# The QKV stage of a fused encoder: rotation of both halves at once on the vector engine, x's norm folded into the head norms, float32 sums, a first weight in parts

## The chip, the core and the metric

The kernel runs on one core of a Trainium2 chip, as one program. Five engines work side by side, each through its own queue in order: TensorE multiplies matrices into PSUM, the vector engine (DVE in the rows) and ScalarE (ACT) work element by element, GpSimd (POOL) does the same more slowly, and SyncE (SP) issues the transfers. They wait for one another by semaphores. The time is that of the device for the whole program in microseconds (us); a profile is one execution, recorded instruction by instruction.

## The reference

The trunk has two layers over 1024 tokens of 1024 features: grouped-query attention and an MLP, then bidirectional gated linear attention and an MLP, and a last norm. The change touches the first step, where q and k are made:

```python
hn = rmsnorm(h, norm_mix[0])                 # y = h * rsqrt(mean(h*h) + EPS) * g
q, k, v = split(hn @ w_qkv)                  # 16 heads of q, 4 of k and v, 64 features each
q = rmsnorm(q.reshape(B, S, 16, 64), q_g)    # over each head's 64 features
k = rmsnorm(k.reshape(B, S, 4, 64), k_g)
# axial rotation: of each 32 features the first 16 are x1, the others x2
rotated = concat([x1 * c - x2 * s, x2 * c + x1 * s])
```

The softmax over q k, its product with v, and everything behind it stay as they are.

## The kernel before

All data are float32. A projection keeps the accuracy by splitting both operands into a high part (`fp32r`, written by a ScalarE cast) and a low part (the difference, on the vector engine): three matmuls, high by high, high by low, low by high (`mm3`, L108 to L111), for each of eight 128-row pieces of the contraction (`proj`, L113), so 24 matmuls of 512 columns. `split` (L95) and `load_w` (L99) make the parts of a weight; `gain_split` (L172) makes those of x with the norm's gain, but without x's root mean square. That factor is one number per token and is put in later.

x lies transposed: features on partitions, tokens along the row, in two halves of 512 tokens. Five tiles of q and k (`qk_tile`, L293), k's four heads first (t = 4) and then four heads of q at a time, each have two weights: one gives the first members of the rotated pairs (`pab[0]`, in the rows `qa`), the other the second (`qb`). So a half-tile is two projections, 48 matmuls, and there are ten half-tiles. For each, ScalarE squares both results, the vector engine adds the squares (`SumSquares`, L137), the sum is split into high and low (`sqh`, `sql`), and two matmuls with the block matrix `blk` (L164, L165) sum over the 32 partitions of each head. `products` (L318) does the rotation's four multiplications, three of them on GpSimd, with tables of cosine and sine that `x_norm` (L225) has already multiplied by x's inverse root. `rotate` (L330) multiplies the head's sum by x's inverse mean square (`xq`, L334), takes the inverse root by logarithm, exponential and one Newton step (`newton`, L124 to L135), multiplies it in (L337), splits the result, and SP writes it to DRAM, from where the score stage reads it.

`rope_late` holds each half-tile's `rotate` back until the next half-tile's projections are issued (`rope_end`, L314), so in TensorE's queue a sum stands behind 48 other matmuls. `hooks` (L232) puts x's norms, the transposes that give the inverse root by token (`by_token`, L182), and v's weights in between. `v_tiles` (L345) then makes v in eight tiles of 24 matmuls of 256 columns, with the last two `rotate` and the first head's maxima (`max_step`, L273) among them. The scores start behind it. The order within each engine's queue is fixed when the program is built, by a scheduler that moves instructions a little against the code; PSUM's banks are four for projections (`a`), two for maxima (`b`), two for sums (`c`).

The same `newton` is used by every norm of the program.

Of the kernel before, what the change touches and what calls it, by code (L numbers as in the profile page):

```python
# [41 lines left out]
NCH = S // P  # L42
LEAD = 22
LAG = 3


C_MIX0, C_MLP0, C_MIX1, C_MLP1, C_FIN, C_QA, C_QB, C_KA, C_KB, C_OUT, NCOL = 0, 8, 16, 24, 32, 40, 41, 42, 43, 44, 46
# [2 lines left out]
def trunk_kernel(tc, xT, wqk, wv, wo, win0, wout0, gqk, gv, gvz, gr, gate, gwo, win1, wout1, cols, rope, cmat, yT):  # L50
# [5 lines left out]
    with ExitStack() as top:  # L56
# [19 lines left out]

        epst = const.tile([P, 1], F32, name="epst")
        nc.vector.memset(epst, EPS)

        PS_BUFS = {"a": 4, "b": 2, "c": 2}  # L80

# [10 lines left out]
        def bank(tag):  # L92
            return psum.tile([P, HN], F32, tag=tag, name="ps_" + tag, bufs=PS_BUFS[tag])
# [27 lines left out]
        def halves(n):  # L121
            return [[None, None] for _ in range(n)]

        def newton(x, n, out=None):  # L124

            w = x.shape[-1]
            r0 = env.tmp.tile([P, HN], F32, tag="rs_r", name="rs_r")[:, :w]
            nc.scalar.activation(out=r0, in_=x, func=AF.Ln, bias=epst, scale=1.0 / n)  # L128
            nc.scalar.activation(out=r0, in_=r0, func=AF.Exp, scale=-0.5)  # L129
            t = env.tmp.tile([P, HN], F32, tag="rs_t", name="rs_t")[:, :w]  # L130
            nc.vector.scalar_tensor_tensor(out=t, in0=r0, scalar=1.0 / n, in1=r0, op0=ALU.mult, op1=ALU.mult)  # L131
            nc.vector.scalar_tensor_tensor(out=t, in0=x, scalar=n * EPS, in1=t, op0=ALU.add, op1=ALU.mult)  # L132
# [59 lines left out]
        with ExitStack() as at:  # L192
# [6 lines left out]
            rx2 = pool.tile([P, 2, HN], F32, name="rx2")  # L199
            rt = const.tile([P, NCH], F32, name="rt")  # L200
            xstack = at.enter_context(ExitStack())
            xpool = pool_of(xstack, "xpool", 16)
            wk = [load_w(wqk[8])]
            for half in range(2):
                for k in range(KT):
                    xr[k][half] = xpool.tile([P, HN], F32, tag="xr", name="xr")
                    nc.sync.dma_start(out=xr[k][half], in_=xT[k][:, HALF[half]])
                if half == 0:
                    wk.append(load_w(wqk[9]))
# [4 lines left out]
            xsums = [SumSquares(nc.vector) for _ in range(2)]  # L214
            wq = [load_w(wqk[i]) for i in range(2)]

            def x_squares(half):
# [12 lines left out]

            x_squares(0)
            x_squares(1)  # L232
# [55 lines left out]
            blk = pool.tile([P, P], F32R, name="blk")  # L288
            blk_f = pool.tile([P, HN], F32, tag="t2", name="blk_f")[:, :P]
            nc.sync.dma_start(out=blk_f, in_=rope[:, 2 * S :])  # L290
            nc.scalar.copy(out=blk, in_=blk_f)

            def qk_tile(t, w=None):  # L293
                w = w or [load_w(wqk[2 * t]), load_w(wqk[2 * t + 1])]
                ga, gb = (C_KA, C_KB) if t == 4 else (C_QA, C_QB)
                for half in range(2):
                    pab = [proj("a", w[i], x, half) for i in range(2)]
                    if hooks:
                        hooks.pop(0)()
                    rope_end()  # L300
                    sums = SumSquares(nc.vector)
                    for ps in pab:
                        sums.add(ps)
                    ab = []
# [5 lines left out]
                    rope_late.append(partial(rotate, t, half, sums, ab, None if t == 4 else products(half, *ab)))  # L310

            rope_late = []

# [1 line left out]
                if rope_late:  # L315
                    rope_late.pop()()

            def products(half, a, b):  # L318
                cc, ss = tabs[:, 0, HALF[half]], tabs[:, 1, HALF[half]]
                out = []  # L320
                for i, (u, v, op) in enumerate(((a, b, ALU.subtract), (b, a, ALU.add))):
                    t1 = pool.tile([P, HN], F32, tag=f"t1{i}", name="t1", bufs=2)
                    t2 = pool.tile([P, HN], F32, tag="t2", name="t2")
# [3 lines left out]
                    out.append(t1)  # L327
                return out

            def rotate(t, half, sums, ab, out):  # L330
                sl = HALF[half]
                out = out or products(half, *ab)
                xq = pool.tile([P, HN], F32, tag="xq", name="xq")
                nc.vector.tensor_tensor(out=xq, in0=sums.total(blk), in1=rx2[:, half], op=ALU.mult)  # L334
                r = newton(xq, 1)
                for i, t1 in enumerate(out):
                    nc.vector.scalar_tensor_tensor(out=t1, in0=t1, scalar=(0.25 if t == 4 else 0.03125), in1=r, op0=ALU.mult, op1=ALU.mult)  # L337
                    hi = pool.tile([P, HN], F32R, tag=f"qo{i}", name="qoh")
                    lo = pool.tile([P, HN], F32R, tag=f"qo{2 + i}", name="qol")
                    split(hi, lo, t1)  # L340
                    dst = kv_dram if t == 4 else q_dram[t]
                    nc.sync.dma_start(out=dst[i, :, sl], in_=hi.bitcast(F32))
                    nc.sync.dma_start(out=dst[2 + i, :, sl], in_=lo.bitcast(F32))

            def v_tiles():  # L345
                for c in range(NCH):
# [928 lines left out]
```

## Time and profile before

| | us |
|---|---|
| timed runs | 2353.15, 2357.78, 2358.01 |
| median | 2357.78 |
| profiled execution | 2352.89 |
| its span, first to last instruction | 2350.8 |
| first score matmul | 178.09 |
| last matmul of the ninth half-tile's sum starts | 140.42 |

The page of the profile shows TensorE busy for 98% of the span, the vector engine 76%, ScalarE 57%, GpSimd 14%. Matmuls overlap, so TensorE's busy time counts some stretches in which it could have taken more; what it really spends per matmul is the distance between two starts. In the fence rows further down, a row of the timeline begins with the start in us and the duration, and a bracket at its end tells how long the engine stood idle before and what released it.

### The profile page before, as it was taken

The page shows a single profiled execution, that of the slowest core. Times are in us where ns is not written, and L with a number is a line of the kernel's source. Part 1 is how long each engine was busy: PE and PEld are TensorE (multiplying, and loading weights), DVE is VectorE, ACT ScalarE, POOL GpSimd, SP SyncE. Part 2 cuts the span into 40 slices and gives each one's busy share as a digit, 9 for nine tenths or more (in the row PEclk, how much of TensorE's full clock was granted, in tenths as well). Part 3 has the DMA queues.
Part 4 walks back from the last instruction along what each step waited for, and adds up shares of the span by engine and source line. Part 5 has one row for each costly group of instructions (what it writes and reads, how often), then busy time and mean ns, then how long its engine had stood idle before and what let it go on. Part 6 is the DMA issues. An engine that isn't in the chain of part 4 may idle for free. (4 is left out here: it accounts for less than half of the span.)

```text
span 2350.8 us, 29858 instructions
## 1 busy us (share of the span) xinstructions
PE 2292.8 (98%) x10710; PEld 1898.6 (81%) x10710; DVE 1777.5 (76%) x2502; ACT 1341.4 (57%) x2386; POOL 333.2 (14%) x267
## 2 busy tenths in 40 slices
PE   8889999999999999999999999999999999999996
PEld 6677777777878888888888888898878888888885
DVE  8999999995786556888776767667696655897785
ACT  7458999994465555433344865655455555543343
POOL 2444444443000000000012000000100000000003
PEclk9999999999999999999999999999999999999998
DMA  4442112104445456954422121125625545965422
GB/s 173 135 146 64 42 41 52 30 14 165 132 160 180 152 175 228 320 166 160 153 99 81 47 74 54 55 72 187 220 91 194 177 152 182 331 204 177 154 89 72
DMA packets 157796, 317.50 MB, mean 135 GB/s; under 512 B 15048, under 2 KB 17872, under 8 KB 157520
## 3 DMA queue, kind: packets, MB, share of 16 engines
q1 hardware_dynamic: 157648, 315.60, 40.2%
q8 instruction: 84, 1.38, 0.2%
q14 instruction: 64, 0.52, 0.1%
HBM read 223.20 MB, written 92.27 MB: 134 GB/s over the span
## 5 line engine op out<-in xcount | busy, mean ns | idle before, releaser
L97 DVE TENSOR_TENSOR wl<-raw,wh 128x1024 fp32r<-128x1024 f32 x293 | 361.0, 1232 | 198.4 <-ACT wh L96 197.0
L96 ACT CAST wh<-raw 128x1024 fp32r<-128x1024 f32 x293 | 307.4, 1049 | 327.7 <-PE ps_a L466 130.6
L96 ACT CAST hh<-hst 128x512 fp32r<-128x512 f32 x224 | 134.9, 618 | 246.1 <-PE ps_a L467 112.4
L147 POOL TENSOR_TENSOR sq<-sq 128x512 f32<-128x512 f32 x35 | 54.6, 1560 | 1373.7 <-ACT sq L145 772.6
L400 POOL TENSOR_TENSOR pl<-p,ph 128x512 fp32r<-128x512 f32 x128 | 178.9, 1397 | 190.4 <-ACT p L397 136.4
L465 PE MATMUL ps_a<-xh,wh 128*128 128x512 f32 x512 | 199.6, 391 | 2.5 <-ACT xh L96 2.5
L467 PE MATMUL ps_a<-xh,wl 128*128 128x512 f32 x512 | 199.8, 391 | 1.8 <-DVE wl L97 1.8
L97 DVE TENSOR_TENSOR hl<-hst,hh 128x512 fp32r<-128x512 f32 x224 | 153.1, 703 | 62.9 <-ACT hh L96 62.1
L466 PE MATMUL ps_a<-xl,wh 128*128 128x512 f32 x512 | 200.5, 392 | 0.0
L465 PE MATMUL ps_a<-hh,wh 128*128 128x512 f32 x512 | 199.3, 389 | 1.1 <-ACT h L505 1.1
L466 PE MATMUL ps_a<-hl,wh 128*128 128x512 f32 x512 | 199.3, 389 | 0.6 <-DVE hl L97 0.6
L467 PE MATMUL ps_a<-hh,wl 128*128 128x512 f32 x512 | 199.2, 389 | 0.0
L396 ACT ACTIVATE ph<-ps_a 128x512 fp32r<-128x512 f32 x248 | 149.0, 601 | 22.2 <-PE ps_a L390 19.7
L397 ACT ACTIVATE p<-ps_a 128x512 f32<-128x512 f32 x256 | 153.1, 600 | 1.0 <-POOL pl L400 0.2
L465 PE MATMUL ps_b<-xh,wh 128*128 128x512 f32 x384 | 149.5, 389 | 0.2 <-DVE s L560 0.2
L467 PE MATMUL ps_b<-xh,wl 128*128 128x512 f32 x384 | 149.4, 389 | 0.0
L466 PE MATMUL ps_b<-xl,wh 128*128 128x512 f32 x384 | 149.4, 389 | 0.0
L277 DVE TENSOR_REDUCE mx<-ps_b 128x1 f32<-128x512 f32 x181 | 121.9, 682 | 7.6 <-PE ps_b L276 5.5
L505 ACT ACTIVATE s<-s 128x512 f32<-128x512 f32 x96 | 60.6, 631 | 105.9 <-DVE s L560 105.9
L465 PEld LDWEIGHTS ps_a<-xh,wh 128*128 128x128 f32 x512 | 96.4, 189 | 23.2 <-ACT xh L96 3.3
L467 PEld LDWEIGHTS ps_a<-xh,wl 128*128 128x128 f32 x512 | 96.5, 188 | 23.1 <-DVE wl L97 2.7
L465 PEld LDWEIGHTS ps_a<-hh,wh 128*128 128x128 f32 x512 | 96.1, 188 | 21.8 <-ACT h L505 1.7
(280 smaller groups left out, 6038.0 us busy)
## 6 DMA issues: line engine op xcount, KB each, us to landing
raw<-in_win_dram SPq DMA_DIRECT2D x80, 512.0 KB, 3.8
raw<-in_wout_dram SPq DMA_DIRECT2D x80, 512.0 KB, 3.9
hst<-hid_dramFalse SPq DMA_DIRECT2D x56, 512.0 KB, 3.8
hst<-hid_dramTrue SPq DMA_DIRECT2D x56, 512.0 KB, 3.5
q<-q_dram SPq DMA_DIRECT2D x96, 128.0 KB, 2.9
hid_dramFalse<-s SPq DMA_DIRECT2D x48, 256.0 KB, 2.1
hid_dramFalse<-t SPq DMA_DIRECT2D x48, 256.0 KB, 3.1
hid_dramTrue<-s SPq DMA_DIRECT2D x48, 256.0 KB, 2.0
```

The source lines that it names most:

```text
L96: nc.scalar.copy(out=hi, in_=src)
L97: (leng or nc.vector).tensor_tensor(out=lo, in0=src, in1=hi.bitcast(F32), op=ALU.subtract)
L147: self.eng.tensor_tensor(out=sq, in0=self.acc, in1=sq, op=ALU.add)
L277: nc.vector.tensor_reduce(out=mx[h][:, half * 8 + c : half * 8 + c + 1], in_=ps, axis=AX.X, op=ALU.max, negate=True)
L396: nc.scalar.activation(out=phh, in_=ps, func=AF.Exp)
L397: nc.scalar.activation(out=p, in_=ps, func=AF.Exp)
L400: (nc.vector if c % 2 == 0 else nc.gpsimd).tensor_tensor(out=pll, in0=p, in1=phh.bitcast(F32), op=ALU.subtract)
L465: nc.tensor.matmul(ps, wh, xh, start=start and i == 0, stop=False, skip_group_check=not start)
L466: nc.tensor.matmul(ps, wh, xl, start=False, stop=False, skip_group_check=not start)
L467: nc.tensor.matmul(ps, wl, xh, start=False, stop=i == len(parts) - 1, skip_group_check=not start)
L505: nc.scalar.activation(out=t, in_=src, func=AF.Relu)
```

## The change

`newton`: the square of the root is taken on ScalarE instead of the vector engine, with an epsilon that can be given. `products` and `rotate`: both members of a pair lie side by side in one tile (`u`, `t1`, `t2`), and each of the two tables multiplies both at once on the vector engine; GpSimd has no part in it. The tables are no longer multiplied by x's norm. Instead of dividing by it, the head's sum gets an added term: 64 times epsilon times x's mean square, in the matmul's sum (`xe`, in two float32r parts, with `ones`). The block sum itself is one float32 matmul on the unsplit squares. Gains take the factors (`gneg`). The two members leave in one transfer per part. At the start, eight matmuls on constants are issued, and k's first weight is loaded and split in four parts of 256 columns between x's first four tiles.

```diff
+WARM = 8
@@
+        epsq = const.tile([P, 1], F32, name="epsq")
+        nc.vector.memset(epsq, EPS * EPS)
+        nc.vector.tensor_scalar_mul(gneg[:, C_QA : C_QB + 1], gneg[:, C_QA : C_QB + 1], 0.125)
@@ newton
-        def newton(x, n, out=None):
+        def newton(x, n, out=None, eps=EPS, bias=epst):
-            nc.scalar.activation(out=r0, in_=x, func=AF.Ln, bias=epst, scale=1.0 / n)
+            nc.scalar.activation(out=r0, in_=x, func=AF.Ln, bias=bias, scale=1.0 / n)
             nc.scalar.activation(out=r0, in_=r0, func=AF.Exp, scale=-0.5)
-            nc.vector.scalar_tensor_tensor(out=t, in0=r0, scalar=1.0 / n, in1=r0, op0=ALU.mult, op1=ALU.mult)
-            nc.vector.scalar_tensor_tensor(out=t, in0=x, scalar=n * EPS, in1=t, op0=ALU.add, op1=ALU.mult)
+            nc.scalar.activation(out=t, in_=r0, func=AF.Square, scale=n ** -0.5)
+            nc.vector.scalar_tensor_tensor(out=t, in0=x, scalar=n * eps, in1=t, op0=ALU.add, op1=ALU.mult)
@@ start
-            wk = [load_w(wqk[8])]
+            warm = bank("c")
+            for _ in range(WARM):
+                nc.tensor.matmul(warm[:, :P], ones_f, ones_f, start=True, stop=True)
+            raw = env.raw.tile([P, D], F32, tag="raw", name="raw")
+            wk = [(wpool.tile([P, D], F32R, tag="wh", name="wh"), wpool.tile([P, D], F32R, tag="wl", name="wl"))]
             for half in range(2):
                 for k in range(KT):
+                    if half == 0 and k < 4:
+                        q = slice(k * 256, k * 256 + 256)
+                        nc.sync.dma_start(out=raw[:, q], in_=wqk[8][:, q])
+                        split(wk[0][0][:, q], wk[0][1][:, q], raw[:, q])
@@ x_squares
-                xsums[half].parts(*[pool.tile([P, HN], F32R, tag=f"qo{2 * half + i}", name="xsq") for i in range(2)])
+                xe[half] = [pool.tile([P, HN], F32R, name=f"xe{half}{i}") for i in range(2)]
+                e = pool.tile([P, 2, HN], F32, tag="t2", name="xe")[:, 0]
+                nc.scalar.activation(out=e, in_=xsums[half].acc, func=AF.Copy, scale=64 * EPS / D)
+                split(*xe[half], e)
+                xsq = pool.tile([P, 2, HN], F32R, tag="qol" if half else "qoh", name="xsq")
+                xsums[half].parts(xsq[:, 0], xsq[:, 1])
@@ x_norm
-                tab = tabs[:, :, HALF[half]]
-                nc.vector.tensor_tensor(out=tab, in0=tab, in1=rx[:, half : half + 1].to_broadcast([P, 2, HN]), op=ALU.mult)
-                nc.scalar.activation(out=rx2[:, half], in_=rx[:, half], func=AF.Square, scale=0.0625)
@@ qk_tile
-                    for ps, g, nm in ((pab[0], ga, "qa"), (pab[1], gb, "qb")):
-                        u = pool.tile([P, HN], F32, tag=nm, name=nm, bufs=2)
-                        nc.scalar.activation(out=u, in_=ps, func=AF.Copy, scale=colt[:, g : g + 1])
-                        ab.append(u)
-                    sums.parts()
+                    u = pool.tile([P, 2, HN], F32, tag="u", name="u", bufs=2)
+                    for i, ps in enumerate(pab):
+                        g = (C_KA if t == 4 else C_QA) + i
+                        nc.scalar.activation(out=u[:, i], in_=ps, func=AF.Copy, scale=gneg[:, g : g + 1])
@@ products
-                for i, (u, v, op) in enumerate(((a, b, ALU.subtract), (b, a, ALU.add))):
-                    (nc.gpsimd if i else nc.vector).tensor_tensor(out=t1, in0=u, in1=cc, op=ALU.mult)
-                    nc.gpsimd.tensor_tensor(out=t2, in0=v, in1=ss, op=ALU.mult)
-                    nc.vector.tensor_tensor(out=t1, in0=t1, in1=t2, op=op)
+                for i, t in enumerate((t1, t2)):
+                    nc.vector.tensor_tensor(out=t, in0=u, in1=tabs[:, i : i + 1, HALF[half]].to_broadcast([P, 2, HN]), op=ALU.mult)
+                nc.vector.tensor_tensor(out=t1[:, 0], in0=t1[:, 0], in1=t2[:, 1], op=ALU.subtract)
+                nc.vector.tensor_tensor(out=t1[:, 1], in0=t1[:, 1], in1=t2[:, 0], op=ALU.add)
@@ rotate
-                nc.vector.tensor_tensor(out=xq, in0=sums.total(blk), in1=rx2[:, half], op=ALU.mult)
-                r = newton(xq, 1)
-                for i, t1 in enumerate(out):
-                    nc.vector.scalar_tensor_tensor(out=t1, in0=t1, scalar=(0.25 if t == 4 else 0.03125), in1=r, op0=ALU.mult, op1=ALU.mult)
-                    split(hi, lo, t1)
+                ps = bank("c")
+                for i in range(2):
+                    nc.tensor.matmul(ps, ones, xe[half][i], start=i == 0, stop=False)
+                nc.tensor.matmul(ps, blk, sums.acc, start=False, stop=True)
+                r = newton(ps, 64, eps=EPS * EPS, bias=epsq)
+                nc.vector.tensor_tensor(out=t1, in0=t1, in1=r[:, None].to_broadcast([P, 2, HN]), op=ALU.mult)
+                split(hi, lo, t1)
```

On the vector engine, one half-tile in the middle of the stage (t = 2). Before, from the sum of its squares to the low parts of the half-tile that is finished meanwhile:

```order
L147 TENSOR_TENSOR sq<-sq 128x512
L326 TENSOR_TENSOR t_1003<-t_1003,t_1004 128x512
L97 TENSOR_TENSOR sql<-sq,sqh 128x512
L131 SCALAR_TENSOR_TENSOR rs_t<-rs_r 128x512
L326 TENSOR_TENSOR t_1008<-t_1008,t_1009 128x512
L132 SCALAR_TENSOR_TENSOR rs_t<-xq,rs_t 128x512
L134 SCALAR_TENSOR_TENSOR rs_t<-rs_t,rs_r 128x512
L337 SCALAR_TENSOR_TENSOR t_892<-t_892,rs_t 128x512
L337 SCALAR_TENSOR_TENSOR t_897<-t_897,rs_t 128x512
L97 TENSOR_TENSOR wl<-raw,wh 128x1024
L97 TENSOR_TENSOR qol<-t_892,qoh 128x512
L97 TENSOR_TENSOR qol<-t_897,qoh 128x512
```

The first product on this engine (L324) and `xq` (L334) stand right in front. Now the like stretch is this (lines are those of the changed kernel):

```order
L152 TENSOR_TENSOR sq<-sq 128x512
L335 TENSOR_TENSOR t_920<-u,tabs 128x1024
L137 SCALAR_TENSOR_TENSOR rs_t<-ps_c,rs_t 128x512
L335 TENSOR_TENSOR t_921<-u,tabs 128x1024
L139 SCALAR_TENSOR_TENSOR rs_t<-rs_t,rs_r 128x512
L336 TENSOR_TENSOR t_920<-t_920,t_921 128x512
L348 TENSOR_TENSOR t_826<-t_826,rs_t 128x1024
L337 TENSOR_TENSOR t_920<-t_920,t_921 128x512
L102 TENSOR_TENSOR wl<-raw,wh 128x1024
L102 TENSOR_TENSOR qol<-t_826,qoh 128x1024
```

The sum's low part is gone, so that the sum of the squares is all that the block matmul needs from this engine.

On TensorE, the tenth and last sum, among the matmuls of the first v tiles. Before, its two matmuls stand some distance apart:

```order
L109 MATMUL ps_a<-wh,xh 128x256
L164 MATMUL ps_c<-sqh,blk 128x512
L110 MATMUL ps_a<-wl,xh 128x256
...
L110 MATMUL ps_a<-wl,xh 128x256
L165 MATMUL ps_c<-sql,blk 128x512
L111 MATMUL ps_a<-wh,xl 128x256
```

Now the norm's two parts (`xe`, here of the second half) and the float32 sum stand together:

```order
L116 MATMUL ps_a<-wh,xl 128x256
L345 MATMUL ps_c<-xe_286,ones 128x512
L345 MATMUL ps_c<-xe_287,ones 128x512
L346 MATMUL ps_c<-sq,blk 128x512
L114 MATMUL ps_a<-wh,xh 128x256
```

All three stand behind the first v tile's 24 matmuls, and the next tile's behind them.

On ScalarE, at the end of the last half-tile (t = 3), now:

```order
L101 CAST qoh<-t_1002 128x1024
L101 CAST wh<-raw 128x1024
L133 ACTIVATE rs_r<-ps_c,epsq 128x512
L150 ACTIVATE sq<-ps_a 128x512
L134 ACTIVATE rs_r<-rs_r 128x512
L321 ACTIVATE u<-ps_a,gneg 128x512
L136 ACTIVATE rs_t<-rs_r 128x512
```

The logarithm of the ninth sum (L133) stands ahead of the last half-tile's second square; before, that square (L145) stood ahead of the logarithm (L128).

## Rows read from the trace of the kernel before

**Rows 1.** Windows: stretch, its length, busy us of PE, PEld, DVE, ACT, POOL, clock, DMA

```profile
0.00:34.95 34.95, 26.96 (x102) 20.92 (x103) 28.22 (x40) 29.07 (x49) 4.94 (x8) 1.00 0.68 243
34.95:140.65 105.70, 96.94 (x410) 78.00 (x410) 99.69 (x118) 53.56 (x87) 45.45 (x27) 0.97 0.39 127
140.65:178.09 37.44, 30.13 (x213) 28.38 (x211) 32.12 (x47) 17.67 (x46) 13.59 (x17) 0.91 0.37 127
```

**Rows 2.** Waits of PE in 34.95 to 140.65: total us, times, longest

```profile
PE ps_c L165 <- DVE sql L97: 5.3, 4, 2.8
PE ps_c L164 <- ACT qoh L96: 1.6, 1, 1.6
PE ps_c L164 <- DVE xq L334: 1.5, 1, 1.5
```

**Rows 3.** Groups by line and form, same stretch: busy us, mean ns, idle before

```profile
L326 DVE TENSOR_TENSOR t<-t,t 128x512 f32<-128x512 f32 x18 | 18.0, 1002 | 5.0 <-POOL t L325 4.8
L325 POOL TENSOR_TENSOR t<-qb,tabs 128x512 f32<-128x512 f32 x9 | 15.6, 1736 | 56.3 <-ACT qb L307 29.9 <-ACT sq L145 14.6 <-DVE tabs L228 9.2
L131 DVE SCALAR_TENSOR_TENSOR rs_t<-rs_r 128x512 f32<-128x512 f32 x10 | 11.2, 1118 | 0.0
L145 ACT ACTIVATE sq<-ps_a 128x512 f32<-128x512 f32 x15 | 8.9, 593 | 0.3 <-PE ps_a L111 0.3
L334 DVE TENSOR_TENSOR xq<-ps_c,rx 128x512 f32<-128x512 f32 x8 | 5.5, 682 | 0.0
L228 DVE TENSOR_TENSOR tabs<-tabs,rx 128x1024 f32<-128x1024 f32 x2 | 2.4, 1222 | 0.0
```

**Rows 4.** Timeline of PE in the tail: start, us, instruction, idle before and releaser

```profile
144.13 0.39 PE L110 MATMUL ps_a<-wl,xh 128*128 128x256 f32 x1 [1.77 <-DVE wl L97]
149.26 0.50 PE L164 MATMUL ps_c<-sqh,blk 128*128 128x512 f32 x1 [3.07 <-ACT sqh L96]
153.46 0.80 PE L165 MATMUL ps_c<-sql,blk 128*128 128x512 f32 x1 [2.24 <-DVE sql L97]
...
178.09 0.39 PE L389 MATMUL ps_a<-q,k 128*128 128x512 f32 x1
```

**Rows 5.** Windows with a lower clock (the number before the DMA share)

```profile
70.00:80.00 10.00, 7.21 (x26) 5.44 (x26) 10.00 (x13) 4.14 (x7) 4.92 (x3) 0.83 0.46 144
...
148.00:162.00 14.00, 10.50 (x63) 9.89 (x64) 12.11 (x17) 5.72 (x17) 7.95 (x8) 0.76 0.35 122
```

**Rows 6.** Timeline of PE around a float32 matmul (L159)

```profile
634.36 0.39 PE L111 MATMUL ps_a<-oh,wl 128*128 128x512 f32 x1
...
637.31 0.39 PE L465 MATMUL ps_a<-xh,wh 128*128 128x512 f32 x1
637.67 1.10 PE L159 MATMUL ps_c<-sq,ones_f 128*128 128x512 f32 x2
...
638.84 0.40 PE L467 MATMUL ps_a<-xh,wl 128*128 128x512 f32 x1
```

**Rows 7.** Timelines of ACT, PE and DVE at the start

```profile
4.58 1.04 ACT L96 CAST wh<-raw 128x1024 fp32r<-128x1024 f32 x1 [2.26 <-DMA raw<-in_wqk_dram]
5.85 0.72 ACT L177 ACTIVATE xh<-xr,colt 128x512 fp32r<-128x512 f32 x1 [0.22 <-DMA xr<-in_xT_dram]
...
6.62 0.79 PE L109 MATMUL ps_a<-xh,wh 128*128 128x512 f32 x1 [6.62 <-ACT xh L177]
...
9.05 0.63 PE L110 MATMUL ps_a<-xl,wh 128*128 128x512 f32 x1
9.48 0.63 PE L111 MATMUL ps_a<-xh,wl 128*128 128x512 f32 x1
...
15.10 1.22 DVE L97 TENSOR_TENSOR wl<-raw,wh 128x1024 fp32r<-128x1024 f32 x1
```

**Rows 8.** DMA issues: KB each, median us from issue to landing

```profile
q<-q_dram SPq DMA_DIRECT2D x96, 128.0 KB, 2.9
...
raw<-in_wqk_dram SPq DMA_DIRECT2D x10, 512.0 KB, 4.0
```

More of the change, by code (lines that the diff above doesn't have):

```diff
@@ L198, in trunk_kernel @@
             rx = pool.tile([P, 2, HN], F32, name="rx")
-            rx2 = pool.tile([P, 2, HN], F32, name="rx2")
             rt = const.tile([P, NCH], F32, name="rt")
@@ L215, in trunk_kernel @@
             wq = [load_w(wqk[i]) for i in range(2)]
+            xe = [None, None]
             def x_squares(half):
@@ L286, in max_end @@
                 nc.sync.dma_start(out=q2[h][64:65].rearrange("p (a b) -> p a b", a=8).bitcast(F32), in_=row.bitcast(F32))
[L288 to L291, printed above, removed]
+            blk = pool.tile([P, P], F32, name="blk")
+            nc.sync.dma_start(out=blk, in_=rope[:, 2 * S :])
             def qk_tile(t, w=None):
                 w = w or [load_w(wqk[2 * t]), load_w(wqk[2 * t + 1])]
-                ga, gb = (C_KA, C_KB) if t == 4 else (C_QA, C_QB)
                 for half in range(2):
@@ L303, in qk_tile @@
                         sums.add(ps)
-                    ab = []
-                    for ps, g, nm in ((pab[0], ga, "qa"), (pab[1], gb, "qb")):
-                        u = pool.tile([P, HN], F32, tag=nm, name=nm, bufs=2)
-                        nc.scalar.activation(out=u, in_=ps, func=AF.Copy, scale=colt[:, g : g + 1])
-                        ab.append(u)
-                    sums.parts()
-                    rope_late.append(partial(rotate, t, half, sums, ab, None if t == 4 else products(half, *ab)))
+                    u = pool.tile([P, 2, HN], F32, tag="u", name="u", bufs=2)
+                    for i, ps in enumerate(pab):
+                        g = (C_KA if t == 4 else C_QA) + i
+                        nc.scalar.activation(out=u[:, i], in_=ps, func=AF.Copy, scale=gneg[:, g : g + 1])
+                    rope_late.append(partial(rotate, t, half, sums, products(half, u)))
             rope_late = []
@@ L316, in rope_end @@
                     rope_late.pop()()
-            def products(half, a, b):
-                cc, ss = tabs[:, 0, HALF[half]], tabs[:, 1, HALF[half]]
-                out = []
-                for i, (u, v, op) in enumerate(((a, b, ALU.subtract), (b, a, ALU.add))):
-                    t1 = pool.tile([P, HN], F32, tag=f"t1{i}", name="t1", bufs=2)
-                    t2 = pool.tile([P, HN], F32, tag="t2", name="t2")
-                    (nc.gpsimd if i else nc.vector).tensor_tensor(out=t1, in0=u, in1=cc, op=ALU.mult)
-                    nc.gpsimd.tensor_tensor(out=t2, in0=v, in1=ss, op=ALU.mult)
-                    nc.vector.tensor_tensor(out=t1, in0=t1, in1=t2, op=op)
-                    out.append(t1)
-                return out
@@ L330, in rotate, with products @@
-            def rotate(t, half, sums, ab, out):
-                sl = HALF[half]
-                out = out or products(half, *ab)
-                xq = pool.tile([P, HN], F32, tag="xq", name="xq")
-                nc.vector.tensor_tensor(out=xq, in0=sums.total(blk), in1=rx2[:, half], op=ALU.mult)
-                r = newton(xq, 1)
-                for i, t1 in enumerate(out):
-                    nc.vector.scalar_tensor_tensor(out=t1, in0=t1, scalar=(0.25 if t == 4 else 0.03125), in1=r, op0=ALU.mult, op1=ALU.mult)
-                    hi = pool.tile([P, HN], F32R, tag=f"qo{i}", name="qoh")
-                    lo = pool.tile([P, HN], F32R, tag=f"qo{2 + i}", name="qol")
-                    split(hi, lo, t1)
-                    dst = kv_dram if t == 4 else q_dram[t]
-                    nc.sync.dma_start(out=dst[i, :, sl], in_=hi.bitcast(F32))
-                    nc.sync.dma_start(out=dst[2 + i, :, sl], in_=lo.bitcast(F32))
+            def products(half, u):
+                t1 = pool.tile([P, 2, HN], F32, tag="t1", name="t1", bufs=2)
+                t2 = pool.tile([P, 2, HN], F32, tag="t2", name="t2")
+                for i, t in enumerate((t1, t2)):
+                    nc.vector.tensor_tensor(out=t, in0=u, in1=tabs[:, i : i + 1, HALF[half]].to_broadcast([P, 2, HN]), op=ALU.mult)
+                nc.vector.tensor_tensor(out=t1[:, 0], in0=t1[:, 0], in1=t2[:, 1], op=ALU.subtract)
+                nc.vector.tensor_tensor(out=t1[:, 1], in0=t1[:, 1], in1=t2[:, 0], op=ALU.add)
+                return t1
@@ new lines, in rotate @@
+            def rotate(t, half, sums, t1):
+                sl = HALF[half]
+                ps = bank("c")
[4 more added lines that the diff above has]
+                nc.vector.tensor_tensor(out=t1, in0=t1, in1=r[:, None].to_broadcast([P, 2, HN]), op=ALU.mult)
+                hi = pool.tile([P, 2, HN], F32R, tag="qoh", name="qoh")
+                lo = pool.tile([P, 2, HN], F32R, tag="qol", name="qol")
+                split(hi, lo, t1)
+                dst = kv_dram if t == 4 else q_dram[t]
+                for i, part in enumerate((hi, lo)):
+                    nc.sync.dma_start(out=dst[2 * i : 2 * i + 2, :, sl].rearrange("i p n -> p i n"), in_=part.bitcast(F32))
```

## The prediction

> **What bounds the kernel now.** The time beside this forecast is that of the profiled execution: 2352.9 us around a span of 2350.8. The timed runs lie at 2353.2, 2357.8 and 2358.0; with the profiled one their mean is 2355.5, and I take the changed kernel to scatter in the same way. A difference of 0.2% (4.7 us) is about what a measurement of this kernel can tell from none.
>
> I read the windows first. They cut the QKV stage into three stretches, up to the first score matmul [rows 1]: the start (to 34.95), eight half-tiles of q and k (34.95 to 140.65), and a tail with the v tiles (140.65 to 178.09). In the middle the vector engine is busy 99.7 of 105.7 us, and so nearly full, while TensorE shows 96.9 of pipelined matmuls. After 178 us TensorE is full and the diff leaves that work as it was, save one step of the root.
>
> Then the matmul's step, since a busy TensorE is not TensorE at its peak. Between 634.36 and 637.31 there are 13 steps of 0.227 us [rows 6]. The middle has 8 x 48 projections at that step (87.1 us), eight sums of two (3.6), x's sum of two (0.45) and eight short transposes (0.9): 92.0 of 105.7 us. So 13.7 us are lost. The largest waits show 8.4 of them [rows 2], all at the sums over a head's features; part of the rest is clock. It fell to its lower level, 1.2 GHz, behind such a wait: the mean granted clock is 0.83 from 70 to 80 us [rows 5], which comes to 3.4 us at half speed and so 1.7 us lost.
>
> Why are the sums late? A 512-element operation of the vector engine takes 682 ns where GpSimd is idle (L334), but L326 and L131 average 1002 and 1118 [rows 3]: they lie beside GpSimd's products of 1736. The vector queue is full, and `sql`, which the sum waits for, stands in it.
>
> In the tail TensorE waits 1.77, 3.07 and 2.24 us [rows 4], and the clock from 148 to 162 us averages 0.76 [rows 5]: 6.7 us of the 14 at half speed, 3.4 lost, of which some 1.2 fall into a wait. That is 9.3 us.
>
> **The change, part by part.**
>
> *Products on the vector engine.* Per half-tile there go from its queue two L326, one L324, L131, L334, `sql`, two L337 and two `qol`; there come two products and the root's multiplication and `qol` over 1024 elements, and two sums of 512. Priced by L228 (1222 ns, 1024 elements, also with a broadcast operand) and L334 (682 ns) [rows 3] the new half-tile is 5 x 1.22 (one weight split among them) + 5 x 0.68 = 9.5 us; the old one showed 99.7 / 8 = 12.5. GpSimd has nothing left there, so the stretched forms go. TensorE then needs 12.4 us for a half-tile (below), so the vector engine has 3 us to spare in each. What is late next is TensorE itself.
>
> *The square on ScalarE.* L145 prices it at 0.59 us [rows 3]. ScalarE then does per half-tile seven operations of 512 (two squares, two scalings, logarithm, exponential, square) at 0.59 to 0.72 (L177, [rows 7]) and two casts of 1024 at 1.04 [rows 7]: some 6.6 us of 12.4, hidden. It adds a wait: L137 on the vector engine waits for this square, and behind it stand the next half's sum and products. ScalarE's square is itself queued behind the logarithm that waits for TensorE's sum. Elsewhere 17 roots make the same exchange at 0.59 for 0.68 (L334's); I book nothing (between 1 us gained and 1 lost).
>
> *Float32 sums.* Two float32r matmuls (0.45 us) are replaced by two on x's norm (0.45) and one in float32. Its price is L159: from 637.31 to 638.84 there stand one step, the float32 matmul in two records, and one step, so 1.53 - 0.45 = 1.08 us [rows 6]. The bounds are two plain steps, 0.45, and the 1.30 that is left if only one step is paid for. This lies on the path: +1.08 in each of ten sums, 10.8 us (4.5 to 13). All of it stands in TensorE's queue, with the next half's 48 matmuls behind.
>
> The Trainium skill (FP8 and Floating Point Precision) counts four passes for true FP32. By that, as an estimate, one costs 0.91 us and the ten sums 9.1; the row asks for more and is what I use.
>
> *Middle.* 92.0 + 8 x 1.08 = 100.6 for 105.7: -5.1 us, if no sum waits. Ends: -10.1 (0.45 each), +8.6 (every wait stays).
>
> *Tail.* The v tiles' second weight and the ninth sum no longer stand behind a full vector queue. 9.3 us won, 1.08 paid for the tenth sum, 1.0 kept for the max reductions, which share the vector engine with the last two half-tiles: -7.2. Ends: -8.8 and +1.1.
>
> *Start.* The first weight comes in four parts between x's first tiles. A weight of 512 KB takes 4.0 us from issue to landing, a transfer of 128 KB 2.9 [rows 8]: the first cast can begin 1.1 us before 4.58, and TensorE near 5.5 instead of 6.62 [rows 7]. The eight warming matmuls need no data and are over by then: a quarter of L159's columns at half speed is 0.54 us, eight are 4.3. If they cost double, the start slips 4 us and this gain is gone. Before, TensorE's first matmuls were 0.43 apart, twice the later step [rows 7], so the clock was low. But the second projection waits for its weight's low part, which ended at 16.3 us [rows 7], behind eight casts and differences of x that both kernels make; the parts add four small casts and three more DMAs in front of it. So I let the 96 matmuls end at 31.5 instead of 32. The first sum then waits for the vector engine, whose queue up to there holds 31 operations of 512 (0.68), three of 1024 (1.22) and four of 256 (some 0.35): 26.2 us from about 3.9, and 1 to 1.5 of stalls, so 31.3. With x's sum (0.45), the norm's (0.45) and 1.08, the block ends at 33.5 instead of 34.95: -1.4 (between -5.7, if nothing but TensorE holds it, and +2).
>
> The Trainium skill (DMA: Bandwidth & Descriptors, Bandwidth) gives 138 GB/s for 64 KB and 341 for 1 MB, a rule against the parts. As an estimate, 512 KB at those rates take 3.8 and 1.5 us: the last part could come 2.3 us late, and the sum would be smaller by that. The medians of 2.9 and 4.0 us [rows 8] speak for the first part and say nothing of the last.
>
> *Sum.* -1.4 - 5.1 - 7.2 = -13.7 us, on 2352.9 for the profiled execution (2339.2), on the mean of 2355.5 that is 2342; I say 2341.
>
> **Rivals.**
>
> *The tail keeps its waits.* The max reductions of the tail, the tables of the last two half-tiles and the last weight splits all stay on the vector engine, and ScalarE's logarithm of the ninth sum stands ahead of the last half's square. If these 9.3 us stay, the tail is +1.1 and the sum -5.4: 2350. For it: TensorE's longest wait, 3.07, lies there and is for ScalarE [rows 4]. Against it: 3 us to spare in each half-tile before.
>
> *Supply doesn't bind the start.* TensorE then runs 96 x 0.227 from 5.5 and the first block ends at 29.3: -5.7, and with a clean tail (-8.2) the sum is -19.0: 2336.5. For it: the clock is up sooner, and the tiles of x may land as fast as they are used. Against it: both helper engines are busy 28 to 29 of the first 35 us [rows 1].
>
> *The waits halve, no more.* The new order puts each half's sum behind the root of an earlier half, so some waits stay. Half of the middle's and the tail's leave +1.8 and -2.6, the start nothing: about -1, 2354.5.
>
> *Slower: the sum's bank.* A sum's bank is now read twice, at last by L137 behind logarithm, exponential and square, and there are two. If a bank is held over 28.6 us, every second sum waits on it, and this eats what the rest wins; at 32 us a half-tile takes 16 instead of 13.2, 22 us in eight, and the kernel is at 2369. Against it: the chain itself is 2.6 us, and one round of both queues adds 16 at most.
>
> **How the numbers follow.** Forecast 52%, start unbound 16, tail waits 18, halved waits 8, slower 6. Faster by over 0.2% are the first three, 0.86; the halved waits are "same", 0.08; 0.06 slower. The forecast's own range is 2334 to 2348 by the scatter of the runs and the price of the float32 matmul. With the unbound start the low end is 2330. Above, it has to take in the tail's rival and reaches 2353; beyond lie the halved waits, in part, and the slower case.
>
> **What would show it.** Right: 34.95 to 140.65 becomes a stretch of some 100.6 us with the vector engine under 80% busy, every operation of 512 near 0.68, no GpSimd product, no wait over 0.5 us at a sum, and no clock under 1.00 there; the float32 sum costs 1.1 us between its neighbours; the first score comes near 164.4 us. Wrong: waits at `sq` or at the bank of the sum, a float32 sum beyond 1.3, a first block later than 35 us, or waits for `wl` and `mx` in the tail. A span after the first score that differs from 2172.7 by more than 2 us would mean that I left something out there.

## The result and the profile after

The changed kernel takes 2340.85 us (median of six runs, 2336.34 to 2342.86), the one before on the same chip 2355.8: a ratio of 0.9935, 95% interval 0.9922 to 0.9947. Timed again later, beside the last kernel of this study, it took 2339.86, 0.9934 (0.9921 to 0.9948). The forecast was 2341.

The windows of the changed kernel, cut where those of before were cut [rows 1]: at the end of the first block, behind the ninth half-tile's sum, and at the first score matmul.

```profile
0.00:36.11 36.11, 33.55 (x119) 24.61 (x119) 28.44 (x45) 28.92 (x50) 5.98 (x8) 1.00 0.69 229
36.11:135.65 99.54, 99.54 (x428) 79.26 (x427) 79.00 (x92) 56.54 (x87) 0.00 (x0) 1.00 0.46 144
135.65:164.74 29.09, 28.70 (x214) 26.92 (x213) 23.52 (x32) 14.89 (x40) 9.12 (x14) 1.00 0.39 141
```

The start grew by 1.16 us (34.95 to 36.11). The middle shrank by 6.16 (105.70 to 99.54), and in it TensorE has no gap, the vector engine is busy 79.00 of 99.54 us, GpSimd does nothing, the clock is 1.00. The tail shrank by 8.35 (37.44 to 29.09). Sum: -13.35, and the first score comes at 164.74 where it was at 178.09.

The groups of the middle, by line and form, answer to [rows 3]:

```profile
L335 DVE TENSOR_TENSOR t<-u,tabs 128x1024 f32<-128x1024 f32 x18 | 21.8, 1221 | 2.5 <-ACT u L321 2.4
L348 DVE TENSOR_TENSOR t<-t,rs_t 128x1024 f32<-128x1024 f32 x8 | 9.8, 1221 | 0.0
L137 DVE SCALAR_TENSOR_TENSOR rs_t<-ps_c,rs_t 128x512 f32<-128x512 f32 x10 | 6.9, 685 | 0.1
L336 DVE TENSOR_TENSOR t<-t,t 128x512 f32<-128x512 f32 x9 | 6.2, 687 | 0.0
L136 ACT ACTIVATE rs_t<-rs_r 128x512 f32<-128x512 f32 x10 | 6.4, 636 | 0.0
```

Every operation of the vector engine on 512 elements takes 0.69 us where L326 and L131 averaged 1.00 and 1.12; one of 1024 takes 1.22, also with a broadcast operand. The waits of TensorE that [rows 2, 4] list are gone. In the middle the view of waits is empty, and in the tail it lists only two short ones for the maxima:

```profile
PE ps_b L300 <- DVE mx L298: 0.2, 1, 0.2
PE ps_b L293 <- DVE mx L294: 0.2, 1, 0.2
```

The timeline of TensorE around a sum in the middle, and at the first score:

```profile
97.56 0.63 PE L345 MATMUL ps_c<-xe,ones 128*128 128x512 f32 x2
98.03 1.02 PE L346 MATMUL ps_c<-sq,blk 128*128 128x512 f32 x2
98.48 0.79 PE L114 MATMUL ps_a<-xh,wh 128*128 128x512 f32 x1
99.11 0.39 PE L115 MATMUL ps_a<-xl,wh 128*128 128x512 f32 x1
...
164.74 0.39 PE L400 MATMUL ps_a<-q,k 128*128 128x512 f32 x1
```

From the float32 sum's start to L115 there are 1.08 us, and they hold the sum and one step of L114 (0.227): the sum costs 0.85, where the forecast had 1.08.

### The profile page after: what moved, and what is told of

Read it like the earlier page. It is cut to its first block, busy times and chain, and to the rows that moved or that the text cites. A ratio compares the mean times of both kernels' runs of the same rounds, so it can differ in the third digit from the quotient of the medians.

```text
span 2341.1 us, 29797 instructions
## 1 busy us (share of the span) xinstructions
PE 2301.9 (98%) x10746; PEld 1905.7 (81%) x10746; DVE 1734.4 (74%) x2448; ACT 1351.3 (58%) x2399; POOL 283.4 (12%) x237
## 4 chain that ended last, share of the span: by engine, by line
PE 79%; DVE 11%; ACT 6%; DMA 1%; issue 1%; POOL 1%; SPq 0%; POOLq 0%; DVEq 0%; ACTq 0%
PE ps_a L477 9%; PE ps_a L478 9%; PE ps_a L476 9%; PE ps_b L477 5%; PE ps_b L476 5%; PE ps_b L478 5%; PE ps_b L116 4%; PE ps_b L115 4%; PE ps_b L114 4%; PE ps_a L116 3%; PE ps_a L114 3%; PE ps_a L115 3%; PE ps_c L477 2%; PE ps_c L478 2%; PE ps_c L476 2%; DVE mx L294 2%
## 5 line engine op out<-in xcount | busy, mean ns | idle before, releaser
L102 DVE TENSOR_TENSOR wl<-raw,wh 128x1024 fp32r<-128x1024 f32 (+2 forms) x296 | 360.0, 1216 | 209.7 <-ACT wh L101 208.6
L101 ACT CAST wh<-raw 128x1024 fp32r<-128x1024 f32 (+2 forms) x296 | 307.8, 1040 | 336.4 <-PE ps_a L477 130.7
```

The source lines that it names most:

```text
L101: nc.scalar.copy(out=hi, in_=src)
L102: (leng or nc.vector).tensor_tensor(out=lo, in0=src, in1=hi.bitcast(F32), op=ALU.subtract)
```

## The experiments

Times are medians; ratios are to the kernel before, timed beside each. Where one run is named, there is one time and no interval, and the reading rests on its profile. The first score is that of the profiled execution.

**The vector engine's products in the old kernel.** GpSimd's products go to the vector engine and nothing else changes, so that the stretching goes and the queue stays long.

```diff
-                    (nc.gpsimd if i else nc.vector).tensor_tensor(out=t1, in0=u, in1=cc, op=ALU.mult)
-                    nc.gpsimd.tensor_tensor(out=t2, in0=v, in1=ss, op=ALU.mult)
+                    nc.vector.tensor_tensor(out=t1, in0=u, in1=cc, op=ALU.mult)
+                    nc.vector.tensor_tensor(out=t2, in0=v, in1=ss, op=ALU.mult)
```

> The kernel before with its three GpSimd products moved to the vector engine and nothing else (the sums stay in two float32r parts, the first weight whole, the tables normalised). Theory A and B (the vector queue then holds 16 x 0.60 + 1.14 = 10.7 us per half-tile against TensorE's 11.3, without stretching): the waits at the sums mostly go and the float32 sums' 10.8 us aren't paid, so the first score comes at 157 to 163 us, earlier than with the whole change (164.7), and the time is 15 to 20 us below before. Rival (the sum without a low part is what freed TensorE): waits for sql stay, first score 174 or later.

Measured: 2352.11 us, 0.9989 (0.998 to 0.9999); first score at 170.36. The ten runs lie between 2347.01 and 2356.91, and the profile is of one near the lower end (2348.13). The expectation was missed: no 15 to 20 us were won. Its waits of TensorE behind 34 us, its windows, and the row of the vector engine on which the longest wait hangs:

```profile
PE ps_c L164 <- ACT sqh L96: 5.3, 1, 5.3
PE ps_a L111 <- DVE wl L97: 4.8, 1, 4.8
...
PE ps_c L165 <- DVE sql L97: 0.6, 2, 0.3
```

```profile
60.00:110.00 50.00, 39.26 (x158) 30.57 (x157) 46.93 (x76) 23.94 (x39) 0.00 (x0) 0.86 0.55 179
87.00:101.00 14.00, 7.04 (x14) 4.43 (x15) 13.68 (x22) 4.40 (x8) 0.00 (x0) 0.51 0.58 184
```

```profile
87.02 0.71 DVE L147 TENSOR_TENSOR sq<-sq 128x512 f32<-128x512 f32 x1
```

No operation is stretched (those of 512 take 0.70), and the queue is still full: 13.68 of 14 us where TensorE stands idle half of the time, and from 87 to 101 us the clock is nearly all at its lower level (0.51). The low part of the squares costs 0.6 us and no more. The longest wait is for the high part, because the sum of the squares itself stood in the vector queue until 87.02, with no idle time before it; the other is for a weight's low part in the same queue. Taking GpSimd out is not enough in the old order.

**Three products back on GpSimd** in the changed kernel, in halves of 512.

```diff
-                for i, t in enumerate((t1, t2)):
-                    nc.vector.tensor_tensor(out=t, in0=u, in1=tabs[:, i : i + 1, HALF[half]].to_broadcast([P, 2, HN]), op=ALU.mult)
+                for i in range(2):
+                    (nc.gpsimd if i else nc.vector).tensor_tensor(out=t1[:, i], in0=u[:, i], in1=tabs[:, 0, HALF[half]], op=ALU.mult)
+                    nc.gpsimd.tensor_tensor(out=t2[:, 1 - i], in0=u[:, 1 - i], in1=tabs[:, 1, HALF[half]], op=ALU.mult)
```

> The changed kernel with three of the four rotation products back on GpSimd (each over 512 elements), everything else as changed. Theory A (GpSimd's products, by stretching the vector engine's operations, made the sums late, and taking them away is what freed them): waits at the sums come back, the stretch between the first and the ninth sum grows from 99.7 us to 105 or more, the first score goes to 170 or later. Theory B (what counts is the sum of the vector queue against TensorE's 12.3 us per half-tile; without xq, the square, sql and the narrow forms it is 6 x 0.60 + 3 x 1.14 + 3 x 1.1 of stretching = 10.3): no waits over 0.5 us at the sums, first score within 2 us of 164.7.

Measured: 2346.5 us, 0.9964 (0.9951 to 0.9977); first score at 171.37, 6.6 us later than the changed kernel's. One wait, with the clock behind it, makes most of that. First the view of waits, then pieces of the chain that ends at the second sum, then two windows:

```profile
PE ps_c L346 <- DVE rs_t L137: 4.4, 1, 4.4
```

```profile
39.12 2.92 POOL t L336 x2
42.05 3.19 POOL vb L384
45.23 1.28 POOL t L335
46.51 1.23 POOL t L336
...
47.77 1.26 DVE t L337
...
49.43 0.68 DVE t L338
50.11 0.61 DVE rs_t L137
...
50.77 1.22 PE ps_c L346 x2
```

```profile
45.00:60.00 15.00, 10.58 (x33) 7.53 (x32) 11.34 (x12) 7.36 (x13) 7.90 (x7) 0.77 0.18 70
60.00:110.00 50.00, 50.00 (x218) 39.94 (x218) 37.24 (x38) 27.36 (x42) 18.55 (x13) 1.00 0.57 174
```

GpSimd fills a constant of v (`vb`, 3.19 us) between its products, and the next ones stand behind it. Sums of products on the vector engine wait for them, L137 stands behind these, and until L137 the sum's bank is held (in this run's line numbers L346 is the norm's matmul, the first into that bank): this is the mechanism of the prediction's slower rival, at one place. The clock falls behind the wait (0.77). From 60 to 110 us nothing on TensorE waits, although GpSimd works 18.55 of 50 us. So in this steady part GpSimd's share costs nothing. It brings nothing either: the vector engine, three products lighter, is busy 37.24 us where the changed kernel is busy 38.68, because L337, which lies beside GpSimd's products, takes 1.76 us in the mean where its twin L338 takes 0.68.

**How much room does the vector engine need?** One of its products is done three times.

```diff
-                for i, t in enumerate((t1, t2)):
+                for i, t in ((0, t1), (1, t2), (1, t2), (1, t2)):
```

> The changed kernel with the second table's product of each half-tile done three times over, so that the vector engine gets 2 x 1.22 = 2.44 us more work per half-tile and nothing else changes. In the middle it is busy 9.6 of 12.25 us; with it 12.1, nearly full, as before the change. Theory (what cleared the sums is the room in the vector engine's queue): with the room gone, waits at the sum or for the norm's chain come back, at least 0.5 us per half-tile, and the first score is at 169 or later. Rival (it is the missing low part of the squares, and the order, that cleared them): the step stays within 0.2 us of 12.25 and the first score within 2 us of 164.7.

Measured: 2343.77 us in one run; first score at 164.22. Windows over three half-tiles, the changed kernel and this one:

```profile
86.20:122.96 36.76, 36.76 (x157) 29.32 (x156) 26.96 (x30) 18.24 (x28) 0.00 (x0) 1.00 0.59 181
```

```profile
86.18:122.94 36.76, 36.76 (x157) 29.29 (x156) 35.50 (x40) 18.26 (x28) 0.00 (x0) 1.00 0.56 170
```

The vector engine is busy 35.50 of 36.76 us instead of 26.96, and the step stays at 12.25. My theory, that room in the queue is what clears the sums, falls in this form; the rival, the missing low part and the new order of the queues, held. One caution: the scheduler also placed an earlier sum elsewhere in TensorE's queue (its matmul starts at 67.79 instead of 73.54).

**The sum again in two parts**, in two steps, since the split squares take the room of the norm's second part. First the norm in one float32r part:

```diff
-                for i in range(2):
-                    nc.tensor.matmul(ps, ones, xe[half][i], start=i == 0, stop=False)
+                nc.tensor.matmul(ps, ones, xe[half], start=True, stop=False)
```

> The changed kernel with x's norm term in one float32r part instead of two: one matmul fewer in each of ten sums. Theory (TensorE is full in the middle, so its queue alone sets the step): 12.25 us per half-tile become 12.02, the first score comes at 162.5 instead of 164.74, no wait at a sum. Rival (the chain over the vector engine and ScalarE sets the step, and TensorE only looks full): the step stays at 12.25, the first score at 164.2 or later, and a wait of some 0.2 us shows at each sum.

Measured: 2339.16 us, 0.9931 (0.9916 to 0.9946); first score at 162.71. Then also the sum:

```diff
+                    sums.parts()
@@
-                nc.tensor.matmul(ps, blk, sums.acc, start=False, stop=True)
+                nc.tensor.matmul(ps, blk, sums.acc[0], start=False, stop=False)
+                nc.tensor.matmul(ps, blk, sums.acc[1], start=False, stop=True)
```

> As the run with one norm part, and the block sum taken again as two float32r matmuls on a high and a low part of the squares, instead of one float32 matmul; the vector engine gets 0.68 us per half-tile back. Theory (the float32 matmul costs 1.08 on the path, and the vector engine has over 2 us to spare in each half-tile without it): 0.63 less in each of ten sums than in that run, a step of 11.4 us, first score near 156.5, no wait over 0.5 us for the parts of the squares. Rival (what cleared the sums is that they no longer wait for the low part, so the float32 matmul is paid for by the waits it removes): waits for the squares' parts come back, the step stays at 12 or more and the first score at 162 or later.

Measured: 2335.12 us, 0.9916 (0.9901 to 0.9931); first score at 160.11. Windows over three half-tiles, of the one and of the other:

```profile
85.39:121.41 36.02, 36.02 (x155) 28.74 (x154) 26.95 (x30) 18.45 (x28) 0.00 (x0) 1.00 0.59 182
```

```profile
84.47:119.21 34.74, 34.74 (x154) 28.72 (x153) 28.42 (x33) 20.29 (x32) 0.00 (x0) 1.00 0.59 185
```

A half-tile takes 12.25, 12.01 and 11.58 us: one float32r matmul less is worth 0.24, and two of them instead of the float32 one 0.43. Behind the first sum no sum waits in either run, so TensorE's queue alone sets the step. The first sum itself waits again for the parts of the squares:

```profile
PE ps_c L346 <- ACT sqh L101: 0.8, 1, 0.8
PE ps_c L347 <- DVE sql L102: 0.5, 1, 0.5
```

That, a wait of 0.7 for a maximum in the tail and above all the smaller price (0.43 instead of 0.63 in each of ten sums) are why 160.11 and not 156.5 came out.

**The float32 sum twice**, for its price by itself.

```diff
+                nc.tensor.matmul(ps, blk, sums.acc, start=False, stop=False)
                 nc.tensor.matmul(ps, blk, sums.acc, start=False, stop=True)
```

> The changed kernel with its float32 block sum issued twice into the same bank (the head norms come out wrong by that). It weighs one float32 matmul by itself, between the same neighbours. Theory A (the prediction's price): 1.08 us more in each half-tile, 12.25 become 13.33, and the first score comes at 175.5. Theory B (from the two runs without it, 12.00 against 11.58 with one float32r matmul more): 0.88 more, 13.13, first score at 173.5.

Measured in one run: 2348.6 us, first score at 172.21; three half-tiles:

```profile
89.76:129.10 39.34, 39.34 (x164) 30.43 (x163) 26.24 (x30) 17.06 (x26) 0.00 (x0) 1.00 0.52 161
```

39.34 / 3 - 12.25 = 0.86 us. Theory B holds; the 1.08 of the prediction falls. The first score came 1.3 us before what B gave; 0.55 of that lies in the start, where the first float32 matmul begins at 34.60 instead of 35.15.

**The start.** First the warming matmuls are left out:

```diff
-            for _ in range(WARM):
-                nc.tensor.matmul(warm[:, :P], ones_f, ones_f, start=True, stop=True)
```

> The changed kernel without the eight warming matmuls; all else stays. Theory 1 (the start is bound by supply): nothing moves, first head sum within 0.5 us of 36.0, first score near 164.7. Rival (the clock): the first sum moves by 1.5 us or more, either way.

Measured: 2338.0 us, 0.9931 (0.9914 to 0.9947); first score at 164.55 (164.74 with them). They are worth nothing that can be seen here. Then the first weight is loaded whole:

```diff
-                        nc.sync.dma_start(out=raw[:, q], in_=wqk[8][:, q])
-                        split(wk[0][0][:, q], wk[0][1][:, q], raw[:, q])
+            wk = [load_w(wqk[8])]
```

> The changed kernel with k's first weight loaded and split whole, as before the change; all else stays. Theory 1 (the start is bound by supply: the parts make x's tiles and the second weight land later, and ScalarE's and the vector engine's queues stand behind them): the first head sum ends near 34 us instead of 36.0, the first score is near 162.7 instead of 164.7, the rest as it was, so some 2 us off the time. Rival (the clock, which rose at 16.3 us instead of 13.2, made the start late): first sum within 0.5 of 36.0, first score 164.7.

Measured: 2339.83 us, 0.9935 (0.992 to 0.995); first score at 163.76, halfway between the two theories. The changed kernel, run again, then showed how far such a difference carries.

> The changed kernel as it is, beside the best version on one chip: 2341, 0.9935 of the kernel before. If its first profile was typical, the span after the first score is 2176; if the 3.6 us more than before came only from drops of the clock, it lies between 2171 and 2177 according to their number.

Measured: 2339.86, as above. Its first block ends at 35.08 and its first score comes at 163.70, both 1.0 earlier than in the first profile of the very same program. So the whole weight's 1.0 us is no more than two executions differ by, and this pair alone shows nothing. All the profiles together show more, since every kernel here begins with the weight either in parts or whole:

| | in parts (8 profiles) | whole (6 profiles, 2 of them of the old arithmetic) |
|---|---|---|
| moved by the DMA engines from 2 to 10 us, GB/s | 253 to 274 | 303 to 327 |
| low part of the second weight starts, us | 15.94 to 17.25 | 14.73 to 15.55 |
| x's sum starts, behind the 96 matmuls of the first block, us | 32.76 to 34.82 | 31.56 to 32.40 |

No row overlaps: the parts slow the transfers and make the first block's matmuls end later, by 1.7 us in the mean. How much of it reaches the first sum depends on the rest. In the run above it began at 34.10, against 35.15 and 34.11 in the two profiles of the changed kernel, because it waited 0.60 us for the squares in the vector queue.

**The best version**: whole weight, one norm part, sum in two parts; first with the warming, then without, then without it once more.

> As the run with the split sums, with the first weight loaded whole as before the change. By the theory that the weight's parts delay the start by 1 us (the run with the whole weight): first score 1.0 earlier than with the split sums alone, near 155.5, and a time of 2331. By the rival (the middle is bound by waits for the split squares): first score at 161 or later, 2337.

Measured: 2334.27 us, 0.9912 (0.9897 to 0.9927); first score at 157.57, 2.5 earlier than with the weight in parts, where 1.0 was expected. Of this, 2.2 stand in the start: the sum's first matmul begins at 33.38 instead of 35.58.

> The same without the eight warming matmuls: whole first weight, one norm part, split sums. If the warming is worth nothing, the first score is within 0.5 us of the run before and the time within 1.5 us of it, near 2330. If warming raises the clock earlier for good, the first score is 1 to 3 us later than in that run, and the time with it.

Measured: 2332.32 us, 0.9905 (0.9889 to 0.9922); first score at 158.00.

> The changed kernel with whole first weight, no warming, one norm part and split sums, again, beside the changed kernel: first score at 158, some 6.7 us earlier than the changed kernel's, and a time of 2333 to 2335, 0.990 of before. If the gain is given back behind the first score, the two times are within 3 us of one another.

Measured: 2331.27 us, 0.9899 (0.9886 to 0.9913), 8.6 us less than the changed kernel timed beside it, whose interval of the ratio lies wholly above. Its windows:

```profile
36.00:132.00 96.00, 96.00 (x440) 79.80 (x439) 83.13 (x99) 60.94 (x97) 0.00 (x0) 1.00 0.51 156
132.00:157.81 25.81, 24.93 (x188) 23.48 (x187) 22.41 (x31) 12.32 (x36) 8.61 (x14) 1.00 0.34 123
```

The first score is 5.9 us earlier than 163.70; the other 2.7 lie behind it and were not traced.

## Why the prediction was right, and where it was not

*Middle: right, with a wrong price in it.* Forecast 100.6, measured 99.54. The step of TensorE's matmuls, the empty list of waits and the vector engine at 79% are as forecast. The mis-sized term is the float32 matmul: 1.08 us in the forecast, 0.86 by doubling it, 0.85 in the timeline, and 0.88 from the run with two parts (0.43 more than two steps of 0.227). Of the 0.22 too much, 0.13 lie in front of it in the row it was read from [rows 6]: from 637.31 to 637.67 are 0.36 us where the step is 0.227. With 0.86 the sum is 92.0 + 8 x 0.86 = 98.9; 0.6 us I did not trace. The Trainium skill (FP8 and Floating Point Precision, TensorE Precision Notes) counts four passes for true FP32, from which I had estimated 0.91. That estimate was nearer than my reading of the row, and the measurement agrees with it to 0.05.

*Why the waits went: half shown.* I named two reasons in one sentence, the stretched operations and the low part standing in a full queue. Without the stretching, the old kernel still waits 5.28 and 4.75 us, and only 0.6 for the low part of the squares; there it was the full queue that held the sum of the squares and a weight. In the new order, the middle does not wait with a full vector engine and no low part (35.50 of 36.76 busy), and not with the low part and room (28.42 of 34.74). So in the new order either of the two, room or a sum without low part, was enough. A full queue together with the low part was run in the old order alone, so the new order itself may be what cleared the sums; that stays open.

*Tail: right.* Forecast -7.2, measured -8.35. The 9.3 us of waits and clock went, the tenth sum cost 0.86, and the 1.0 kept for the maxima was not needed (two waits of 0.2).

*Start: wrong sign.* Forecast -1.4, measured +1.16 in the first profile and +0.13 in the second (35.08). A first block later than 35 us was one of the signs of being wrong that I had named. Two terms failed, "1 to 1.5 of stalls" in the vector queue and the 96 matmuls that were to end at 31.5. The vector engine, ScalarE and TensorE in the first profile of the changed kernel:

```profile
3.88 0.43 DVE L102 TENSOR_TENSOR wl<-raw,wh 128x256 fp32r<-128x256 f32 x1 [0.94 <-ACT wh L101]
5.29 0.75 DVE L185 SCALAR_TENSOR_TENSOR xl<-xr,colt,xh 128x512 fp32r<-128x512 f32 x1 [0.98 <-ACT xh L182]
...
7.27 0.75 DVE L185 SCALAR_TENSOR_TENSOR xl<-xr,colt,xh 128x512 fp32r<-128x512 f32 x1 [0.89 <-ACT xh L182]
9.09 0.42 DVE L102 TENSOR_TENSOR wl<-raw,wh 128x256 fp32r<-128x256 f32 x1 [1.07 <-ACT wh L101]
10.23 0.75 DVE L185 SCALAR_TENSOR_TENSOR xl<-xr,colt,xh 128x512 fp32r<-128x512 f32 x1 [0.72 <-ACT xh L182]
...
17.15 1.22 DVE L102 TENSOR_TENSOR wl<-raw,wh 128x1024 fp32r<-128x1024 f32 x1
...
24.92 2.07 DVE L102 TENSOR_TENSOR wl<-raw,wh 128x1024 fp32r<-128x1024 f32 x1
...
29.53 0.69 DVE L152 TENSOR_TENSOR xr<-xr 128x512 f32<-128x512 f32 x1 [0.49 <-ACT xe L237]
...
34.41 0.69 DVE L152 TENSOR_TENSOR sq<-sq 128x512 f32<-128x512 f32 x1
```

```profile
8.65 0.41 ACT L101 CAST wh<-raw 128x256 fp32r<-128x256 f32 x1 [1.42 <-DMA raw<-in_wqk_dram]
```

```profile
5.30 0.80 PE L114 MATMUL ps_a<-xh,wh 128*128 128x512 f32 x1 [0.47 <-ACT xh L182]
...
33.98 0.39 PE L169 MATMUL ps_c<-xsq,ones 128*128 128x512 f32 x1
...
34.45 0.63 PE L345 MATMUL ps_c<-xe,ones 128*128 128x512 f32 x2
35.15 1.13 PE L346 MATMUL ps_c<-sq,blk 128*128 128x512 f32 x2
```

TensorE began at 5.30, as forecast (5.5). Behind 3.88 the vector engine stood idle 0.98 + 0.89 + 1.07 + 0.72 + 0.49 = 4.15 us instead of 1 to 1.5. Another 0.9 is work above the 26.2 booked: two stretches, of which the 2.07 is one, lie beside GpSimd's fills for v. So the squares' sum ended at 35.10, not 31.3. Of these 3.8 us, 1.2 was saved, mostly because x's sum and the norm's (0.9) were already done when it came. But TensorE was hardly earlier: x's sum, behind the 96 matmuls, began at 33.98 (32.93 in the second profile) instead of 31.5, the norm's two steps from 34.45 ended at 34.90, and the float32 sum began at 35.15. Both chains were late, and the vector engine's was last by a quarter of a microsecond. Behind the idle time stand transfers, which the parts slow (the table above): the third weight part's cast waited 1.42 us for its data. In the second profile of the same kernel it did not:

```profile
7.13 0.41 ACT L101 CAST wh<-raw 128x256 fp32r<-128x256 f32 x1
...
9.20 0.41 ACT L101 CAST wh<-raw 128x256 fp32r<-128x256 f32 x1 [0.46 <-DMA raw<-in_wqk_dram]
```

The second weight's low part starts at 17.15 and, in the second profile, at 16.11, where it stood at 15.10 before [rows 7]: 2.05 and 1.01 us late. The Trainium skill (DMA: Bandwidth & Descriptors, Bandwidth) has smaller transfers move fewer bytes per us, and from its two rates, of transfers issued from GpSimd where SP issued these, I had estimated up to 2.3 us for the last part. No row here times that part alone; the 253 to 274 GB/s against 303 to 327 go the way that the page says. I had the rule in front of me and booked nothing for it.

A rival is the clock: TensorE's steps were 0.43 apart until 16.22 in the first profile, and until 12.89 before. By their length that is the lower level, though the windows show 1.00 there; in the run with the whole weight, steps of 0.43 stand in a window of 0.56 (8 to 10 us). The clock may be part of the first profile's loss, but it is not the whole: in the second profile the steps are 0.23 from 11.93 on, earlier than before, and x's sum still begins at 32.93 where it began at 31.96.

*Behind the first score* the span is 2176.4 us in the first profile and 2174.4 in the second, against 2172.7 before: beyond the 2 us that I had allowed, once. One thing differs between the two profiles, in a stretch that the change leaves alone:

```profile
660.00:680.00 20.00, 17.98 (x72) 14.11 (x71) 17.10 (x24) 10.75 (x18) 0.00 (x0) 0.91 0.52 176
```

```profile
660.00:680.00 20.00, 17.99 (x78) 14.28 (x77) 17.49 (x24) 11.75 (x19) 0.00 (x0) 1.00 0.58 188
```

A clock of 0.91 over 20 us is 3.6 us at half speed, 1.8 lost, six matmuls fewer. TensorE waits there in both, 1.12 and 0.90 us in the first profile, 1.11 and 0.90 in the second; only in the first does the clock then fall. A second such fall (0.89 from 1230 to 1245 us) also lies in the first profile alone. Together they would explain more than the 2.0 us between the two. The remaining 1.7 against before is not explained, and it is not the clock: summed over windows of 10 us behind the first score, the lower level cost 8.4 us in the second profile and 8.3 before (12.1 in the first).

*The result* came out at the forecast in part by luck: the start's loss (2.6 us worse than forecast) was met by the middle and the tail (1.1 and 1.2 better).

## What to carry to other kernels

When one engine is full and another waits for one of its results, fewer and wider operations on the full one and one operand less in the waiting chain are two cures; try each alone, since here, in the new order, either was enough. Before a rewrite replaces two cheap matmuls with one dear one to spare the other engine, look again once that engine has room: here the two cheap ones were worth 0.43 us in each of ten sums. Price an instruction by doubling it, or from a row whose neighbours stand at the normal step, and book a stall for transfers that are cut smaller in a stretch where the engines behind them are already full: here four parts for one weight made the first block's matmuls end 1.7 us later.

## What the runs showed that I had not expected

- The start of one program differs by 1.0 us between two executions (first block at 36.11 and 35.08), so a single profile cannot judge an edit there that is worth no more; eight profiles against six could.
- An earlier first matmul did not by itself end the block earlier: it stood at 5.30 and 5.54 in the two profiles of the changed kernel, and at 6.62 before, and x's sum began at 33.98, 32.93 and 31.96.
- A vector engine busy for 97% of a stretch (35.50 of 36.76 us) need not hold anybody up.
